# Spreading softmax gates over experts: gate folded into ScalarE's one-hot, the other one-hot built for four tokens in one VectorE compare

## The chip, the cores and the metric

The kernel is one program on one core of a Trainium2 chip. The metric is device time in microseconds (us) of one execution. TensorE (PE) does the products, VectorE (DVE), ScalarE (ACT) and GpSimd (POOL) the elementwise work and the gathers, and SyncE (SP) issues most of the transfers.

## The reference, cut to what matters

The layer mixes tokens (a gated recurrence beside a convolution) and then runs a layer of 16,384 single-neuron experts. Only the second half touches the change:

```python
sc, idx = lax.top_k(s, PEER_TOPK)                 # per head two lists of 16 keys out of 128
cand = (sc[:, :, 0, :, None] + sc[:, :, 1, None, :]).reshape(T, PEER_HEADS, 256)
top_sc, pos = lax.top_k(cand, PEER_TOPK)          # 16 experts i * 128 + j per head
eidx = jnp.take_along_axis(cidx, pos, axis=-1)
gate = jax.nn.softmax(top_sc, axis=-1)
...
act = jax.nn.gelu(jnp.einsum('thkd,td->thk', u_tab[eb], hb), approximate=False)
y   = jnp.einsum('thk,thkd->td', gb * act, v_tab[eb])
```

1,024 tokens, 8 heads, 16 experts per head: 128 (expert, gate) pairs for each token. All other input shapes are 1,024 features wide.

## The kernel before

**Two ways through the experts.** The 1,024 tokens are 8 blocks of 128. Blocks 3 and 7 (`GATHERED`) fetch their experts' rows by indirect DMA. Blocks 0, 1, 2, 4 and 5 (`DENSE`) compute all experts with matrix products and multiply the result by a dense table of gates. Block 6 (`MIXED`) gathers the rows of the first table, and its gates, already multiplied by the gelu, are spread like those of the dense blocks for the second product. The dense part goes over all 128 groups of experts in two passes: tokens of blocks 0 to 2 first, then 4 to 6.

**Spreading.** `spread` turns the 128 pairs (i, j, gate) of each token of a block into a dense table `wd[.., j, i, token]`. It transposes the three lists so that the pair is on the partition and the token in the free dimension (`tr`: part 0 is i, part 1 is j, part 2 is the gate). Then, for four tokens at a time (a group; 32 groups per block), it builds two one-hot matrices [pair, 128] for each token: `oj` on ACT (line 989: the distance |iota - j|; line 992: Relu(1 - distance), once for all four tokens) and `oi` on DVE (line 990: compare iota with i, times the gate, once per token). PE multiplies them (line 982), into one PSUM bank (`gps`) for the four tokens; ACT copies the bank into `wt` (line 974), and after four groups SP sends `wt` to `wd` in DRAM (line 976). `oj` and `oi` have two buffers each, `wt` has one. The dense part reads `wd` back eight expert groups at a time (`wgrp`, line 1161).

**Order.** Spreading is work beside the main work: a generator that emits a group per step, and `tick` calls a fraction of a step between matrix products (`RATE_PICK`, `RATE_PICK_END`). Its instructions get a later priority (`LATER`), and a scheduler with its own estimate of durations then fixes the order on each engine. At run time every engine executes its list in order. Blocks 0 to 2 are spread while the second half of the tokens is in the recurrence, the convolution's output, the merge, the second norm and the query products; blocks 4, 5 and then 6 are spread during the first dense pass. The first dense pass may not read `wd` before all of blocks 0 to 2 stand in it (`side.until`).

**The dense part's own needs.** For every group of experts ACT and DVE split two weight tiles into a high and a low part (lines 301 and 302), ACT takes the gelu out of the only `ups` bank (line 1086), DVE multiplies it by the gates (line 1091), and PE runs 24 products into `ups` and 6 per token block into `y` (lines 1078 to 1080, 1108 to 1112).

Of the kernel before, what the change touches and what calls it, by code (L numbers as in the profile page):

```python
# [8 lines left out]
F32 = mybir.dt.float32  # L9
# [4 lines left out]
AF = mybir.ActivationFunctionType  # L14
OP = mybir.AluOpType
# [66 lines left out]
class Side:  # L82
    """Work emitted a few steps at a time between the steps of other work, and how urgent it is beside that."""
# [38 lines left out]
def layer_kernel(tc, a, out):  # L122
# [18 lines left out]
    def tick():  # L141
        """A step of the work beside, its vector instructions kept behind the main work of a few steps ago."""
        code = nc.cur_bb.bb.instructions
        n = len(code)
        for i in range(n - 1, seen[0] - 1, -1):
            if code[i].engine == mybir.EngineType.DVE:
                beats.append(code[i].name)
                break
        side.tick()
        if len(beats) == BEATS:  # L150
            for ins in code[n:]:
                if ins.engine == mybir.EngineType.DVE:
                    tc.add_manual_dep(ins, beats[0], mybir.DependencyInfo(
                        mybir.DependencyClass.NoSync, mybir.DependencyReason.DATA), reason="pace")
        rec.tick()
        norm.tick()
        tail.tick()
        due[0] = min(due[0] + TAP_RATE, 2.0)
        work_taps(int(due[0]))
        due[0] -= int(due[0])  # L160
        seen[0] = len(code)

    ctx = ExitStack()
    with ctx:
# [13 lines left out]
        def bank():  # L178
            """A PSUM bank for side work."""
            turn[0] += 1  # L180
            return spare[turn[0] % len(spare)].tile([P, 4, P], F32, name="gps")

# [23 lines left out]
        def rstd_of(ssq, n, scale, tag):  # L206
            """1 / sqrt(scale * ssq + EPS): a first guess from the exponent, then Newton steps."""
            m = small.tile([P, n], F32, name=tag + "m")
            nc.vector.tensor_scalar(m, ssq, -0.5 * scale, -0.5 * EPS, op0=OP.mult, op1=OP.add)
            t = small.tile([P, n], F32, name=tag + "t")  # L210
            r = small.tile([P, n], F32, name=tag + "r")
            ti, ri = t.bitcast(I32), r.bitcast(I32)
            nc.vector.tensor_single_scalar(ti, m.bitcast(I32), 1, op=OP.arith_shift_right)
            nc.vector.tensor_scalar(ri, ti, -1.0, float(0x5F3759DF - (1 << 30) - (1 << 22)), op0=OP.mult, op1=OP.add)
            for _ in range(3):
                nc.vector.tensor_mul(t, m, r)
                nc.vector.tensor_mul(t, t, r)
                nc.vector.scalar_tensor_tensor(r, t, 1.5, r, op0=OP.add, op1=OP.mult)
            return r

        # lower bounds of the forget gates
# [18 lines left out]
        def ada(js, cols=None):  # L240
            """Parts js of the conditioning: as rows in DRAM, or with features on the partitions of cols."""
# [62 lines left out]
        def transpose_split(pp, src, hi, lo, b):  # L304
            """src [tokens, features] -> token block b of hi, lo [feature, k, tokens]."""
            for k0 in range(0, KB, 4):
                ps = pp.tile([P, 4, P], F32, name="hps")
                for k in range(4):
                    nc.tensor.transpose(ps[:, k], src[:, P * (k0 + k):P * (k0 + k + 1)], ident)
                d = (slice(None), slice(k0, k0 + 4), slice(P * b, P * b + P))  # L310
                split(hi[d], lo[d], ps)
# [12 lines left out]
        class Mm:  # L324
            """Products with streamed weights, 256 columns at a time, in two halves of the contraction."""
# [38 lines left out]
            def weights(self, name, i):  # L364
                """The planned weights that come next; those after them are made ready a product later."""
                if not self.ready:
                    self.prepare()
                n, j, r = self.ready.popleft()
                assert (n, j) == (name, i)
                self.ahead = not self.ready  # L370
                return r

            def mm3(self, ps, l, r, step):
                """ps = sum over k of l(part, k)^T r(part, k) in three exact-product passes."""
                for k in range(KB):
                    nc.tensor.matmul(ps, l(0, k), r(0, k), start=k == 0, stop=False)
                    nc.tensor.matmul(ps, l(0, k), r(1, k), start=False, stop=False)
                    nc.tensor.matmul(ps, l(1, k), r(0, k), start=False, stop=k == KB - 1)
                    if k % step == step - 1:
                        tick()  # L380
                if self.ahead:
                    self.ahead = False
                    self.prepare()

            def feat(self, w, m, act):
                """Output features 128 m.. on partitions, tokens free."""
# [6 lines left out]
            def halves(self, w, act):  # L393
                """As feat for both m, the first half of the tokens first."""
# [7 lines left out]
            def tok(self, ws, bs, act):  # L402
                """Tokens of block b on partitions, 256 output features, for (w, b) of ws, bs."""
# [6 lines left out]
        def normed(M, where, raw):  # L410
            """The normalised input, features on partitions."""
# [14 lines left out]
        def modulate(raw, u, cols):  # L426
            """The modulated input in two parts."""
# [15 lines left out]
        def conv_in(M, cp, u, g):  # L443
            """The gated input of the convolution; its taps are left to be worked off later."""
# [29 lines left out]
        def conv_norm(M, cp, c):  # L474
            """Layer norm and swish of the convolution's output for a chunk, in DRAM."""
# [37 lines left out]
        def parts(where, src, c, name):  # L513
            """A chunk of src in two parts."""
# [22 lines left out]
        def merge(M, where, c, mg):  # L537
            """The gated sum of the branches for a chunk: mg, in two parts."""
# [15 lines left out]
        def out_norm(M, c, mg, u2):  # L554
            """The first residual sum of a chunk, and its norm and modulation: u2, in two parts."""
# [41 lines left out]
        def project(M, hp, g, u):  # L597
            """q, f, v and the output gate of two heads for a chunk, in turn."""
# [25 lines left out]
        def recurs(M, hp, c, u, between):  # L624
            """The recurrence for a chunk, two heads at a time; the last ones are left as work beside."""
# [12 lines left out]
        def recur(M, hp, g, c, z, scanm):  # L638
            """The recurrence of two heads over a chunk's tokens, its norm and gate."""
# [18 lines left out]
            # the diagonal of the scores, and zeros elsewhere  # L658
# [13 lines left out]
            # from each even token to the next: the same sums on all partitions  # L672
# [15 lines left out]
            # within each group of 2h tokens: from its first half to its second  # L688
# [21 lines left out]
            # q exp(b) in qk, k exp(b_last - b) in e  # L710
# [53 lines left out]
            # per-head norm, gate, back to features on partitions  # L764
# [25 lines left out]
        def topk(vals, idx, src, work):  # L790
            """The 16 largest of src's rows in order, and where they stand."""
# [6 lines left out]
        def ask(M, c, u2):  # L798
            """Query projection, key scores and the top 16 of each list, for a chunk."""
# [25 lines left out]
        def select(sp, b, sv, si):  # L825
            """The lists i, j of the block's experts i * 128 + j and their gates: [tokens, heads * 16]."""
# [31 lines left out]
            # which row and column of the candidates' triangle each place is  # L858
# [7 lines left out]
            def lookup(dst, one, x, hs):  # L866
                """sum over a of one[a] * (list x's entry a)"""
# [46 lines left out]
        def line():  # L914
            """A tile as long as a token's features."""
# [9 lines left out]
        def gather_u(b):  # L925
            """gate * gelu(u . h) with the rows of peer_u gathered for each token."""
# [17 lines left out]
        def gather_v(b):  # L944
            """The block's weighted rows of peer_v, gathered for each token."""
# [14 lines left out]
        def spread(sp, b, ij, w):  # L960
            """wd[.., j, i, token] = sum of w over the token's experts i * 128 + j."""
# [4 lines left out]
            nc.vector.tensor_copy(tr, ps[:, :3])  # L966
            yield
            hot = out_ = wt = None
            for n in range(P // 4 + 2):
# [14 lines left out]
                if n < P // 4:  # L984
                    oj = sp.tile([P, 4, P], F32, name="oj", bufs=2)
                    oi = sp.tile([P, 4, P], F32, name="oi", bufs=2)
                    for x in range(4):
                        t = 4 * n + x
                        nc.scalar.activation(oj[:, x], iota, AF.Abs, bias=tr[:, 1, t:t + 1], scale=-1.0)
                        nc.vector.tensor_scalar(oi[:, x], iota, tr[:, 0, t:t + 1], tr[:, 2, t:t + 1],  # L990
                                                op0=OP.is_equal, op1=OP.mult)
                    nc.scalar.activation(oj, oj, AF.Relu, bias=1.0, scale=-1.0)
# [7 lines left out]
        def pick(res):  # L1000
            """Side work: from the top lists of all blocks to the dense weights of their experts."""
# [19 lines left out]
        def gather():  # L1021
            """Side work: what is gathered for each token."""
# [14 lines left out]
        def dense(fc, gathers):  # L1037
            """All experts in turn for the tokens of a pass, weighted by wd: their rows of peer_v, summed in PSUM."""
# [23 lines left out]
            def tokens(p):  # L1062
                """Features of the tokens of pass p."""
# [6 lines left out]
            def dots(s):  # L1070
                """u . h of the experts i * 128 .. (on partitions)."""
# [50 lines left out]
            def close():  # L1122
                """The last steps, a block of tokens after the other, and what follows them."""
# [171 lines left out]
def prepare(i):  # L1295
    """The arrays as the kernel reads them, and constants that depend on shapes alone."""
# [47 lines left out]
```

## Time and profile before

| what | value |
|---|---|
| median of 3 runs | 3755.42 us (3749.34 to 3763.02) |
| span of the profiled execution | 3746.1 us |
| median of the runs above that span | 9.3 us |
| PE busy | 3610.6 us, 96% |
| DVE busy | 3157.9 us, 84% |
| ACT busy | 1849.1 us, 49% |
| spreading, first line 990 to last | 1169.3 to 2668.3 us |

The runs' times include what lies around the span; no separate time of the profiled execution is recorded, so its own time is taken as the span, and the step to the runs is the 9.3 us in the table. Busy times are unions: instructions of one engine overlap by about a tenth of a microsecond, so busy time over count is less than the mean duration of one. A PE that is shown busy is not at its peak rate, but it waits for nobody. The granted clock (PEclk) is given as a share of full speed: 1.00 is 2.4 GHz, and a lower mean of a window means that part of it ran at 1.2 GHz.

### The profile page before, as it was taken

To read this page: it belongs to the slowest core of one execution; us is meant where nothing else is said; L and a number is where in the kernel's file an instruction comes from. 1 tells how busy PE (TensorE), PEld (TensorE's weight loads), DVE (VectorE), ACT (ScalarE), POOL (GpSimd) and SP (SyncE) were. 2 spreads that over 40 slices of the span, in tenths; PEclk is the share of its full clock that TensorE was granted. 3 is DMA by queue.
4 is the path that set the end of the run, shared out by engine and by line. 5 is a ranking of instruction groups with operands and counts; after the bars stand their busy time and mean duration, and the time that the engine had idled before them with its cause. 6 is when DMAs were issued, how large, how long until landed. Compare 5 with 4: busy or idle time off the path is not lost. (4 is left out here: it accounts for less than half of the span.)

```text
span 3746.1 us, 57252 instructions
## 1 busy us (share of the span) xinstructions
PE 3610.6 (96%) x20610; PEld 3203.6 (86%) x20610; DVE 3157.9 (84%) x6739; ACT 1849.1 (49%) x3260; POOL 779.3 (21%) x652
## 2 busy tenths in 40 slices
PE   8999999899999999999999999999998999999997
PEld 5888888778899879988888899999987888888886
DVE  4999989967899966789898888898888888778888
ACT  4111355523467877644444566666534444444443
POOL 0000000000000100013333434343333333233332
PEclk9999999899999999999999999999999999999999
DMA  5222477468444778778788999999999999999996
GB/s 230 79 79 90 152 257 258 168 211 316 164 144 152 241 279 318 270 264 285 261 275 287 345 324 330 332 344 355 332 328 327 328 333 344 316 330 340 328 340 214
DMA packets 371405, 999.44 MB, mean 267 GB/s; under 512 B 30376, under 2 KB 142504, under 8 KB 360112
## 3 DMA queue, kind: packets, MB, share of 16 engines
q1 hardware_dynamic: 278960, 660.19, 50.5%
q0 software_dynamic: 92160, 335.59, 25.3%
q8 instruction: 162, 2.65, 0.3%
q14 instruction: 123, 1.01, 0.1%
HBM read 864.57 MB, written 131.09 MB: 266 GB/s over the span
## 5 line engine op out<-in xcount | busy, mean ns | idle before, releaser
L921 POOL DMA_INDIRECT gt<-in_peer_u_dram,ei x384 | 465.2, 1211 | 2139.1 <-ACT o L759 947.2
L1078 PE MATMUL ups<-u,uhi 128*128 128x384 f32 (+1 forms) x2048 | 637.8, 311 | 12.8 <-ACT act L1086 12.8
L1079 PE MATMUL ups<-u,uhi 128*128 128x384 f32 (+1 forms) x2048 | 636.2, 311 | 2.4 <-DMA u<-u2s 2.4
L1080 PE MATMUL ups<-u,ulo 128*128 128x384 f32 (+1 forms) x2048 | 635.9, 311 | 0.0
L1108 PE MATMUL y<-vhi,whi 128*128 128x512 f32 x1524 | 587.0, 394 | 12.0 <-ACT whi L301 8.0
L1109 PE MATMUL y<-vlo,whi 128*128 128x512 f32 x1524 | 589.9, 393 | 1.6 <-DVE vlo L302 1.5
L937 DVE SCALAR_TENSOR_TENSOR gt<-gt,ut 128x1024 f32<-128x1024 f32 x384 | 466.3, 1219 | 63.9 <-DMA gt<-in_peer_u_dram,ei 58.6
L1112 PE MATMUL y<-vhi,wlo 128*128 128x512 f32 x1524 | 465.7, 392 | 5.9 <-DVE wlo L302 5.9
L301 ACT ACTIVATE uhi<-uraw 128x512 fp32r<-128x512 f32 x512 | 309.9, 625 | 227.0 <-PE ups L1079 177.5
L921 POOL DMA_INDIRECT gt<-in_peer_v_dram,ei x256 | 313.1, 1223 | 515.5 <-DVE yg L953 459.9
L1078 PEld LDWEIGHTS ups<-u,uhi 128*128 128x128 f32 x2048 | 390.0, 190 | 25.6 <-ACT act L1086 16.1
L302 DVE TENSOR_TENSOR ulo<-uraw,uhi 128x512 fp32r<-128x512 f32 x512 | 346.0, 687 | 78.0 <-ACT uhi L301 76.1
L302 DVE TENSOR_TENSOR vlo<-vraw,vhi 128x1024 fp32r<-128x1024 f32 x256 | 312.8, 1222 | 110.8 <-ACT vhi L301 109.8
L1079 PEld LDWEIGHTS ups<-u,uhi 128*128 128x128 f32 x2048 | 390.1, 190 | 12.3 <-DMA u<-u2s 3.1
L1080 PEld LDWEIGHTS ups<-u,ulo 128*128 128x128 f32 x2048 | 389.8, 190 | 0.3
L301 ACT ACTIVATE vhi<-vraw 128x1024 fp32r<-128x1024 f32 x256 | 270.2, 1056 | 234.7 <-PE y L1112 140.7
L1108 PEld LDWEIGHTS y<-vhi,whi 128*128 128x128 f32 x1524 | 287.3, 189 | 68.6 <-ACT whi L301 11.4
L1112 PEld LDWEIGHTS y<-vhi,wlo 128*128 128x128 f32 x1524 | 284.9, 188 | 69.3 <-DVE wlo L302 11.0
L1109 PEld LDWEIGHTS y<-vlo,whi 128*128 128x128 f32 x1524 | 286.4, 189 | 55.2 <-DVE vlo L302 2.4
L953 DVE SCALAR_TENSOR_TENSOR yg<-gt,gate,yg 128x1024 f32<-128x1024 f32 x254 | 324.7, 1278 | 5.6 <-DMA gt<-in_peer_v_dram,ei 5.4
L301 ACT ACTIVATE whi<-wgrp 128x384 fp32r<-128x384 f32 x256 | 133.7, 522 | 352.4 <-DVE wgrp L1091 315.7
L469 DVE SCALAR_TENSOR_TENSOR y<-gl,convw,y 128x1024 f32<-128x1024 f32 x240 | 292.8, 1277 | 0.3
(298 smaller groups left out, 7460.9 us busy)
## 6 DMA issues: line engine op xcount, KB each, us to landing
uraw<-in_peer_uT_dram SPq DMA_DIRECT2D x256, 512.0 KB, 6.4
vraw<-in_peer_v_dram SPq DMA_DIRECT2D x256, 512.0 KB, 6.1
raw<-in_w_in_dram SPq DMA_DIRECT2D x96, 512.0 KB, 5.0
wd<-wt SPq DMA_DIRECT2D x48, 1024.0 KB, 6.7
wgrp<-wd SPq DMA_DIRECT2D x32, 1536.0 KB, 14.0
adaw<-in_ada_w_dram SPq DMA_DIRECT2D x24, 1024.0 KB, 8.1
raw<-in_wq_dram SPq DMA_DIRECT2D x32, 512.0 KB, 5.2
raw<-in_w_b_dram SPq DMA_DIRECT2D x16, 512.0 KB, 4.3
```

The source lines that it names most:

```text
L301: nc.scalar.activation(hi, src, AF.Copy)
L302: nc.vector.tensor_sub(lo, src, hi.bitcast(F32))
L469: nc.vector.scalar_tensor_tensor(ys[0], gl[:, j:j + S], convw[:, cb, j:j + 1], ys[0], op0=OP.mult, op1=OP.add)
L921: nc.gpsimd.indirect_dma_start(out=gt, out_offset=None, in_=a[table], in_offset=bass.IndirectOffsetOnAxis(ap=ei[:, j:j + 1], axis=0))
L937: nc.vector.scalar_tensor_tensor(gt, gt, 1.0, ut, op0=OP.mult, op1=OP.mult, accum_out=act[:, j:j + 1])
L953: nc.vector.scalar_tensor_tensor(y, gt, w[:, j:j + 1], y, op0=OP.mult, op1=OP.add)
L1078: nc.tensor.matmul(o, hi[:, k], u2[kh][:, 0, k, :m], start=kh + k == 0, stop=False)
L1079: nc.tensor.matmul(o, hi[:, k], u2[kh][:, 1, k, :m], start=False, stop=False)
L1080: nc.tensor.matmul(o, lo[:, k], u2[kh][:, 0, k, :m], start=False, stop=kh + k == 4)
L1108: nc.tensor.matmul(ys[x][dh], whi[:, r], vhi[:, c], start=first, stop=False)
L1109: nc.tensor.matmul(ys[x][dh], whi[:, r], vlo[:, c], start=False, stop=False)
L1112: nc.tensor.matmul(ys[x][dh], wlo[:, r], vhi[:, c], start=False, stop=last)
```

## The change

In `spread`, for the blocks outside `MIXED`, the second one-hot `oi` no longer carries the gate. It is a pure compare, built for the four tokens by one DVE instruction whose two inputs are broadcast (iota over the tokens, i over the 128 columns). The gate moves into `oj`: in place of one Relu(1 - d) over 128x512, ACT does four Relu(gate - gate * d) over 128x128, each with a bias and a scale read from a column of an SBUF tile (`tr[:, 2]` and the new tile `neg`, which one DVE instruction per block fills with the negated gates). The gates of those blocks are softmax values and thus positive, so the Relu still cuts every column but the right one. Block 6 keeps the old form, since its gates may be negative.

```diff
             nc.vector.tensor_copy(tr, ps[:, :3])
+            neg = sp.tile([P, P], F32, name="neg")
+            nc.vector.tensor_scalar(neg, tr[:, 2], -1.0, None, op0=OP.mult)
             yield
...
                     for x in range(4):
                         t = 4 * n + x
                         nc.scalar.activation(oj[:, x], iota, AF.Abs, bias=tr[:, 1, t:t + 1], scale=-1.0)
-                        nc.vector.tensor_scalar(oi[:, x], iota, tr[:, 0, t:t + 1], tr[:, 2, t:t + 1],
-                                                op0=OP.is_equal, op1=OP.mult)
-                    nc.scalar.activation(oj, oj, AF.Relu, bias=1.0, scale=-1.0)
+                    if b in MIXED:
+                        for x in range(4):
+                            t = 4 * n + x
+                            nc.vector.tensor_scalar(oi[:, x], iota, tr[:, 0, t:t + 1], tr[:, 2, t:t + 1],
+                                                    op0=OP.is_equal, op1=OP.mult)
+                        nc.scalar.activation(oj, oj, AF.Relu, bias=1.0, scale=-1.0)
+                    else:
+                        for x in range(4):
+                            t = 4 * n + x
+                            nc.scalar.activation(oj[:, x], oj[:, x], AF.Relu, bias=tr[:, 2, t:t + 1],
+                                                 scale=neg[:, t:t + 1])
+                        nc.vector.tensor_tensor(oi, iota[:, None, :].to_broadcast([P, 4, P]),
+                                                tr[:, 0, 4 * n:4 * n + 4, None].to_broadcast([P, 4, P]), op=OP.is_equal)
                     hot = oj, oi, 4 * n
```

The diff also empties comment and docstring lines, which changes nothing that runs.

## Rows read from the trace of the kernel before

**Rows 1.** The page: busy time, share of the span, instructions of each engine.

```profile
PE 3610.6 (96%) x20610; PEld 3203.6 (86%) x20610; DVE 3157.9 (84%) x6739; ACT 1849.1 (49%) x3260; POOL 779.3 (21%) x652
```

**Rows 2.** Windows, the two stretches that spread: length, busy time by engine, clock, DMA.

```profile
1169.00:1613.00 444.00, 421.49 (x2814) 385.44 (x2814) 349.80 (x1203) 341.25 (x756) 28.88 (x28) 0.97 0.72 256
2000.00:2680.00 680.00, 668.46 (x3697) 613.46 (x3696) 585.42 (x1096) 429.21 (x926) 269.96 (x213) 0.99 0.93 330
```

**Rows 3.** Waits of PE, 1160 to 2700 us: total, times, longest.

```profile
PE gps L982 <- ACT oj L992: 12.2, 7, 5.0
...
PE gps L982 <- ACT wt L974: 6.5, 2, 6.3
PE y L1112 <- DVE wlo L302: 5.9, 9, 1.2
...
PE gps L982 <- DVE oi L990: 2.1, 1, 2.1
```

**Rows 4.** Groups by line, 1169 to 1613 us: count, busy, mean ns, idle before.

```profile
L989 ACT ACTIVATE oj<-iota,tr 128x128 f32<-128x128 f32 x384 | 121.8, 392 | 8.9 <-DVE tr L966 4.7 <-PE gps L982 4.0
L992 ACT ACTIVATE oj<-oj 128x512 f32<-128x512 f32 x96 | 58.6, 624 | 0.2
L974 ACT ACTIVATE wt<-gps 128x512 f32<-128x512 f32 x96 | 55.4, 589 | 45.5 <-PE gps L982 25.6 <-DMA wd<-wt 19.9
...
L990 DVE TENSOR_SCALAR oi<-iota,tr 128x128 f32<-128x128 f32 x384 | 106.3, 345 | 33.9 <-PE gps L982 33.7
```

**Rows 5.** Groups by line and shape: ACT with and without a bias from SBUF.

```profile
L508 ACT ACTIVATE sq<-cv,vecs 128x512 f32<-128x512 f32 x16 | 11.1, 714 | 1.4 <-DVE cv L509 1.0 <-DVE cv L506 0.4
...
L491 ACT ACTIVATE sq<-cv 128x512 f32<-128x512 f32 x16 | 9.4, 621 | 3.5 <-PE hps L492 3.5
```

**Rows 6.** The same view: a DVE operation of two tensors, one input broadcast.

```profile
L694 DVE TENSOR_TENSOR e<-bc 128x512 f32<-128x512 f32 x48 | 32.9, 685 | 0.1
```

**Rows 7.** Windows of 20 us: PE, PEld, DVE, ACT, POOL busy, clock, DMA.

```profile
1220.00:1240.00 20.00, 20.00 (x173) 20.00 (x172) 17.54 (x49) 19.94 (x38) 4.54 (x4) 1.00 0.52 175
1240.00:1260.00 20.00, 12.28 (x93) 11.66 (x92) 18.37 (x45) 19.68 (x40) 3.97 (x4) 0.85 0.83 280
1260.00:1280.00 20.00, 20.00 (x124) 17.21 (x123) 19.32 (x47) 18.14 (x44) 4.39 (x4) 0.98 0.84 296
1280.00:1300.00 20.00, 19.67 (x133) 17.72 (x132) 20.00 (x44) 16.36 (x35) 2.09 (x2) 1.00 0.71 244
1300.00:1320.00 20.00, 20.00 (x143) 18.41 (x142) 17.20 (x33) 10.75 (x20) 1.69 (x1) 1.00 0.55 191
1340.00:1360.00 20.00, 12.87 (x68) 11.41 (x68) 8.23 (x29) 17.27 (x46) 0.00 (x0) 0.74 0.82 285
2060.00:2080.00 20.00, 13.68 (x61) 11.93 (x60) 10.46 (x21) 6.39 (x14) 4.41 (x5) 0.83 0.90 344
```

**Rows 8.** The same windows, ACT's line 992 alone: busy time, count (one per group).

```profile
1220.00:1240.00 20.00, 2.48 (x4) 1.00 0.52 175
1240.00:1260.00 20.00, 3.10 (x5) 0.85 0.83 280
1260.00:1280.00 20.00, 3.76 (x6) 0.98 0.84 296
1280.00:1300.00 20.00, 3.04 (x5) 1.00 0.71 244
1300.00:1320.00 20.00, 1.14 (x2) 1.00 0.55 191
```

**Rows 9.** Groups by line, 2000 to 2680 us: the distances of the later blocks.

```profile
L989 ACT ACTIVATE oj<-iota,tr 128x128 f32<-128x128 f32 x384 | 121.8, 391 | 21.7 <-PE gps L982 18.7 <-DVE tr L966 2.9
```

**Rows 10.** Waits over the whole span: around the transfer of `wt`.

```profile
ACT wt L974 <- DMA wd<-wt: 45.6, 20, 8.6
```

**Rows 11.** Timeline of SP: the first read of `wd` by the dense part.

```profile
1616.54 0.38 SPq L1161 DMA_DIRECT2D wgrp<-wd  x1
```

## The prediction

> **What bounds the kernel now.** I read the page first: PE is busy for 96% of the span, DVE for 84%, ACT for 49% [rows 1]. By these averages moving work from DVE to ACT looks like good balance, and PE decides the time. But an average over a program of many stages says little about two of them, so next I read windows over the stretches in which spreading runs: 1169 to 1613 us (blocks 0 to 2) and 2000 to 2680 us (blocks 4, 5, 6). In the first PE is busy for 421.5 of 444 us, DVE for 349.8 and ACT for 341.3, in the second PE for 668.5 of 680, DVE for 585.4 and ACT for 429.2 [rows 2]. So in the first stretch ACT isn't an idle engine at 49%: it is at 77%, about level with DVE. Windows of 20 us show more: from 1220 to 1260 us ACT is busy for 19.9 and 19.7 of 20 us, while DVE is at 17.5 and 18.4 [rows 7].
>
> Third, the waits of PE, since only what delays PE can move the end. From 1160 to 2700 us the largest wait of PE for another engine is for ACT's `oj` (12.2 us in 7 waits), then the copy to `wt`, also ACT (6.5 us). DVE's `oi` made it wait once, for 2.1 us [rows 3]. So the engine that is relieved is hardly waited for in spreading, and the engine that gets the work is.
>
> **The change, part by part.** 5 blocks of 32 groups take the new form: 160 groups, 96 in the first stretch (384 instructions of line 990 there, four per group [rows 4]) and 64 of the 96 groups in the second [rows 9].
>
> *DVE, removed and added.* Four compares per group are busy for 106.3 us over 384, 0.277 us each, 1.11 us per group [rows 4]. In their place stands one operation of two tensors over 128x512; the nearest row has one broadcast input and takes 0.685 us [rows 6]. The trace has none with both inputs broadcast; between no extra and the whole old price, I take the row. Saved per group: 1.11 - 0.685 = 0.42 us; 41 us in the first stretch, 27 in the second, 67 in all. Nothing at all would be saved at 1.11 us. `neg` adds five DVE operations over 128x128 for these blocks and one for block 6; at a compare's 0.277 us [rows 4] that is 1.7 us in all, and the saving covers it; without that cover it would be 1.7 us of DVE.
>
> *ACT, removed and added.* One Relu over 128x512 is busy for 58.6 / 96 = 0.610 us [rows 4]. The four new ones over 128x128 are like the distances of line 989, which read a bias from SBUF: 121.8 / 384 = 0.317 us each [rows 4]. But they also read their scale from SBUF, and no row has both. What one such operand costs is to be seen: the same shape takes 714 ns with a bias from SBUF and 621 without [rows 5], 0.093 us. So a new Relu costs between 0.317 (the second operand is free) and 0.410 us. I take the upper end, since the first operand's price was paid in full. Added per group: 4 x 0.410 - 0.610 = 1.03 us; at the lower end 4 x 0.317 - 0.610 = 0.66.
>
> The Trainium skill ("ScalarE: Activation LUTs", section "What ACT_TABLE_LOAD costs") says that each pointer operand of an ACTIVATE adds about 93 ns; for the second one no run here shows it, and by the page the sum would be the upper end.
>
> In all ACT gets 160 x 1.03 = 165 us more (106 at the lower end), against the 67 that DVE is spared.
>
> *Where the added work lies.* In the second stretch 64 x 1.03 = 66 us go into an ACT that is idle for 680 - 429 = 251 us [rows 2]. What hides it is PE's own pace; if ACT had no room there, it would be 66 us. PE's gelu bank is single, so a gelu that waits behind the Relus may still cost something: I put 1 us (0 to 4).
>
> In the first stretch 96 x 1.03 = 99 us meet 444 - 341.3 = 102.7 us of idle ACT [rows 2], and 45.5 us of that idle time are waits for PE and for the `wt` transfer [rows 4]. ACT would be full. At the lower end it is 63 us, and ACT is at 91%. Nor is the room where the work is. From 1220 to 1300 us ACT is idle for 0.06 + 0.32 + 1.86 + 3.64 = 5.9 us [rows 7], and 4 + 5 + 6 + 5 = 20 groups are in these windows [rows 8]. 20 x 1.03 = 20.6 us of added work leave ACT 14.7 us behind at 1300 us (20 x 0.66 = 13.2, and 7.3 behind, at the lower end). From 1300 to 1320 there are 9.25 us of idle time and 2 groups [rows 7, 8], so 7.2 us are made up, and the rest in the later windows.
>
> What queues behind the added instructions on ACT: the evictions of the recurrence's and the convolution's products and the splits of weights, for which PE waits, and the copy to `wt`, for which SP's transfer to `wd` waits and behind it, in SP's order, the loads of weights. `wt` has one buffer, and its copies already waited 45.6 us for transfers [rows 10]; each time ACT now has more to catch up on.
>
> How much of the 14.7 us reaches PE? Between nothing and all. Nothing, if the scheduler lets spreading slip behind the main work, which its later priority allows; the added work would then only have to be done before the dense part first reads `wd` at 1616 us [rows 11]. All, if PE's list keeps its products of `oj` and `oi` where they are. For a value between, the trace has a hint: from 1220 to 1260 us ACT was full and PE still waited by name for `oj` for only a part of the idle 7.7 us of 1240 to 1260 [rows 7]. So the scheduler copes in part. I take half, 7 us.
>
> *What DVE's relief gives back.* PE's waits for DVE in this whole stretch are those for `wlo` and `oi`, 5.9 + 2.1 us [rows 3]. The second goes at best, and part of the first: 0 to 5 us, and I take 1, since PE's main waits have other causes.
>
> *Removed dependences.* A product now waits for one compare of all four tokens, and for a Relu of its own token; before it was the other way round. The first product may start 0.2 us sooner after ACT's work begins, the last one 1.03 us later. That is within the 7 us.
>
> **Sum.** +7 +1 -1 = +7 us against the profiled span: 3746.1 + 7 = 3753 us. The median of the runs lies 9.3 us above that span, so the same step from it gives 3755.4 + 7 = 3762 us, 0.2% more. A measurement here can tell about 0.3% (11 us) from no change, so the forecast is "no change that can be told", leaning to slower.
>
> The Trainium skill ("ScalarE: Activation LUTs", section "Rules for kernel authors") says that Relu, products and the like belong on VectorE rather than ScalarE. By that rule the whole move is for the worse, which is the first rival; the trace bears it out in that a one-hot piece takes 0.277 us on DVE and 0.317 or more on ACT [rows 4].
>
> **Rivals.** *Slower, because ACT becomes the bound of the first stretch.* Place: 1220 to 1520 us. All 14.7 us reach PE, and an idle PE also loses clock: in 1240 to 1260 us 7.7 idle us go with a mean clock of 0.85, 0.15 x 20 = 3 us of full speed lost; in 1340 to 1360 us 7.1 with 0.74, 5.2 us [rows 7]. At 0.4 us per idle us, 14.7 becomes 20.6, plus 1 for the second stretch: 3755.4 + 22 = 3777 us. It decides from about 8 us of new idle time in PE (8 x 1.4 = 11). For it speaks that ACT's added work fills the stretch's idle time, against it that spreading may slip and that PE's named waits for `oj` were small when ACT was full.
>
> *Faster, because DVE was what held the first stretch.* DVE is at 17.5 to 20.0 of 20 us from 1220 to 1300 [rows 7], and 20 groups there free 20 x 0.42 = 8.4 us. If that lets the chains through DVE run ahead, the idle time and the clock lost in 1240 to 1260 go, 7.7 + 3 = 11 us, and a few of the 6.3 idle us at 2060 to 2080 [rows 7]: 14 us in all, 3755.4 - 14 = 3741 us. Against it: DVE's `oi` was waited for 2.1 us only [rows 3], and the stall at 1340 to 1360 came with DVE busy for 8.2 of 20 us. But any change of the instructions lets the scheduler place everything anew, and the stalls at 1340 and at 2060, worth 12 and 10 us with their lost clock, can go or others appear.
>
> *The change doesn't do what it says.* If a compare with two broadcast inputs took 1.1 us or more, DVE would gain nothing and ACT would still pay: the -1 goes, 3763 us, which isn't told from the forecast.
>
> **Chances and range.** Forecast, with the last rival: 0.44. Slower by more than 11 us: 0.36. Faster by more than 11 us: 0.20, mostly for the placing anew. The likeliest case's own range is 3748 to 3767 us (the unknown operand price and the share that reaches PE, 0 to 8 us of stall with its clock). The range to hold the time 8 times in 10 takes in both others: 3742 to 3786 us; the upper end is for the 14.7 us in full and as much again from the later waits around `wt`, 3755.4 + 1 + 2 x 14.7.
>
> **What the profile after would show.** If the prices are right: Relu of 128x128 at about 0.48 us in its mean (392 + 93 ns), 160 compares of 128x512 at about 0.69 us, DVE's busy time down by some 65 us and ACT's up by 165. If the mechanism is right: ACT at over 95% from 1169 to 1613 us, PE's waits for `oj` above the 12.2 us of before, in the first stretch, and none of note after 2100 us, where PE keeps its pace. Wrong would be: spreading that is finished at the same time with ACT well below full (the second operand is free), PE's idle time in the first stretch smaller than 444 - 421.5 = 22.5 us [rows 2], or a change of time that arises where nothing is spread.

## The result, and the profile after

| kernel | median of the runs (lowest to highest) | ratio to the kernel before, 95% interval |
|---|---|---|
| before | 3752.38 us (3745.97 to 3763.02, 4 runs) | |
| after | 3784.73 us (3782.84 to 3786.45, 4 runs) | 1.0081 [1.0063, 1.0099] |

The change costs 32 us, 0.8%. The span of the profiled execution is 3784.3 us, 38.2 us above that of before. The runs of the kernel after take 1.8 us more than their span. By that step the profiled execution of before took about 3748 us, some 4 us under its kernel's median here, so a few of the 38.2 belong to it and not to the change. The 9.3 us between its span and the median of its runs are mostly this difference between executions.

The page after, the row that answers to [rows 1]:

```profile
PE 3636.3 (96%) x20610; PEld 3224.1 (85%) x20610; DVE 3102.5 (82%) x6265; ACT 2001.2 (53%) x3738; POOL 771.7 (20%) x652
```

ACT has 152 us more and DVE 55 us less. The groups by line after, 1169 to 1650 us, which hold all 96 groups of blocks 0 to 2 as the shorter window of [rows 4] does:

```profile
L1001 ACT ACTIVATE oj<-oj,tr,neg 128x128 f32<-128x128 f32 x384 | 162.7, 488 | 1.4 <-DVE neg L968 1.4
...
L991 ACT ACTIVATE oj<-iota,tr 128x128 f32<-128x128 f32 x384 | 123.3, 395 | 13.5 <-PE gps L984 12.4 <-DVE tr L966 1.1
L1003 DVE TENSOR_TENSOR oi<-iota,tr 128x512 f32<-128x512 f32 x96 | 65.7, 686 | 54.8 <-PE gps L984 54.5 <-issue 0.2
L976 ACT ACTIVATE wt<-gps 128x512 f32<-128x512 f32 x96 | 55.6, 588 | 20.3 <-PE gps L984 16.8 <-DMA wd<-wt 3.5
```

A folded Relu is busy for 162.7 / 384 = 0.424 us, the compare for 0.684. The prices are close to the forecast ones. Note the window: before, the last of these groups ended at 1611 us, now at 1650.

The windows after. The first and third answer to [rows 2]:

```profile
1169.00:1613.00 444.00, 418.40 (x2704) 380.40 (x2703) 304.67 (x869) 402.22 (x959) 32.69 (x28) 0.95 0.70 251
1613.00:1660.00 47.00, 33.96 (x168) 29.08 (x166) 31.30 (x147) 39.17 (x96) 4.03 (x3) 0.78 0.54 195
2000.00:2680.00 680.00, 671.04 (x3695) 616.55 (x3694) 564.53 (x928) 487.69 (x1106) 252.87 (x207) 0.99 0.92 327
```

The window of the kernel before for the second of these rows:

```profile
1613.00:1660.00 47.00, 43.85 (x226) 39.76 (x225) 42.17 (x170) 20.90 (x32) 7.74 (x8) 1.00 1.01 329
```

The third row after is as good as before (671.0 busy, 668.5 before), although ACT has 58 us more in it. In the first, PE is idle for only 3 us more, but at a lower granted clock (0.95, before 0.97), and it got through 2704 matrix products where it had done 2814. Then comes a stretch with 13 idle us and a granted clock of 0.78, where the kernel before had 3 and 1.00. PE's waits after, 1160 to 1700 us (total, times, longest):

```profile
PE gps L984 <- ACT oj L1001: 15.5, 15, 4.6
PE gps L984 <- DVE oi L1003: 5.8, 2, 3.8
PE ups L1090 <- ACT act L1098: 3.6, 1, 3.6
PE acc L376 <- ACT qt L811: 3.2, 1, 3.2
PE gps L984 <- ACT wt L976: 2.6, 2, 2.3
```

Named waits for `oj` grew by 3.3 us only [rows 3]. They can't explain 32 us. What does is seen when three moments are laid beside each other: the end of the main work (the last copy of a query product, `qt`), the end of spreading for the first pass (the 96th copy to `wt`), and the start of the dense part (its first gelu, `act`). The timeline of ACT before (start, duration, what, idle time before it in brackets):

```profile
1610.92 0.60 ACT L974 ACTIVATE wt<-gps 128x512 f32<-128x512 f32 x1 [0.30 <-PE gps L982]
...
1616.40 0.60 ACT L811 ACTIVATE qt<-acc 128x512 f32<-128x512 f32 x1 [1.58 <-PE acc L378]
...
1622.35 0.49 ACT L1086 ACTIVATE act<-ups 128x384 f32<-128x384 f32 x1
```

The timeline of ACT after; its first two rows are the last copies of blocks 0 and 1:

```profile
1346.55 0.60 ACT L976 ACTIVATE wt<-gps 128x512 f32<-128x512 f32 x1 [1.68 <-PE gps L984]
...
1501.08 0.60 ACT L976 ACTIVATE wt<-gps 128x512 f32<-128x512 f32 x1
...
1625.36 0.60 ACT L811 ACTIVATE qt<-acc 128x512 f32<-128x512 f32 x1 [0.95 <-PE acc L378]
...
1649.98 0.60 ACT L976 ACTIVATE wt<-gps 128x512 f32<-128x512 f32 x1 [0.53 <-PE gps L984]
...
1659.85 0.49 ACT L1098 ACTIVATE act<-ups 128x384 f32<-128x384 f32 x1
```

Before, spreading ended 5.5 us ahead of the main work, and the dense part began 6 us behind the main work. After, the main work is 9 us later, but spreading ends 24.6 us behind it, and the dense part's first gelu comes 9.9 us behind spreading.

What held the dense part is seen at its first product on PE (`ups`). The timeline of PE before:

```profile
1616.20 0.33 PE L1078 MATMUL ups<-u,uhi 128*128 128x384 f32 x1
```

The timelines of PE and of DVE after:

```profile
1650.63 0.69 PE L1090 MATMUL ups<-u,uhi 128*128 128x384 f32 x1 [0.69 <-ACT wt L976]
...
1664.15 0.56 DVE L1103 TENSOR_TENSOR wgrp<-wgrp,act 128x384 f32<-128x384 f32 x1 [3.44 <-DMA wgrp<-wd]
```

Before, this product came right behind the main work's last ones, 4.7 us after spreading's last copy had ended (1610.92 + 0.60 us). After, PE stood idle until that copy was through (1649.98 + 0.60) and began 0.05 us behind it. So it isn't the gates in `wd` that the dense part waited for at its start: they are first used at 1664.15 us, 4.3 us after the first gelu had begun. PE's list has the dense part's first product behind spreading's last group.

The dense part starts 37.5 us later, and from there to the end of the span the two profiled executions take the same time (2123.7 us before, 2124.5 after).

### The profile page after: what moved, and what is told of

It reads as the page before. It is cut to its first block, busy times and chain, and to the rows that moved or that the text cites. A ratio compares the mean times of both kernels' runs of the same rounds, so it can differ in the third digit from the quotient of the medians.

```text
span 3784.3 us, 57277 instructions
## 1 busy us (share of the span) xinstructions
PE 3636.3 (96%) x20610; PEld 3224.1 (85%) x20610; DVE 3102.5 (82%) x6265; ACT 2001.2 (53%) x3738; POOL 771.7 (20%) x652
## 5 line engine op out<-in xcount | busy, mean ns | idle before, releaser
L937 DVE SCALAR_TENSOR_TENSOR gt<-gt,ut 128x1024 f32<-128x1024 f32 x384 | 466.5, 1220 | 68.9 <-DMA gt<-in_peer_u_dram,ei 68.2
```

The costliest lines, as they stand in the source:

```text
L937: nc.vector.scalar_tensor_tensor(gt, gt, 1.0, ut, op0=OP.mult, op1=OP.mult, accum_out=act[:, j:j + 1])
```

## The experiments

Times are medians of runs. There were three sets, each on a chip of its own with the kernel before beside it (medians of 3753.66, 3758.60 and 3755.28 us), and each ratio is taken within its set. For each the three moments were read from ACT's timeline of its profiled execution, each from the first copy of a query product on (901.3 us before, 902.4 to 908.2 in the others), so that what differs in the hundreds of microseconds ahead of spreading is left out. The table gives how much later than in the kernel before each comes; "rest" is the change of the time from the first gelu to the end of the span.

| kernel | ratio | block 0 spread | block 1 | block 2 | main work | first gelu | rest |
|---|---|---|---|---|---|---|---|
| before (us from the first copy) | | 415.5 | 553.2 | 709.6 | 715.1 | 721.1 | 2123.7 |
| after | 1.0081 | +28.7 | +45.5 | +37.9 | +7.8 | +36.3 | +0.8 |
| e2, new form in blocks 0 to 2 | 1.0115 | +26.8 | +42.7 | +35.0 | +5.1 | +33.4 | +11.4 |
| e8, in blocks 0 and 1 | 1.0111 | +28.2 | +48.0 | +38.9 | +10.3 | +37.0 | +9.3 |
| e7, in block 0 | 1.0043 | +22.6 | +15.8 | +17.9 | +2.1 | +14.9 | +14.8 |
| e1, in blocks 4 and 5 | 1.0041 | -4.0 | -5.3 | +0.3 | +3.5 | +3.4 | +2.5 |
| e4, the fold alone | 1.0110 | +26.7 | +40.8 | +37.3 | +9.5 | +35.1 | +12.6 |
| e3, the merged compare alone | 1.0033 | +9.2 | +7.9 | +9.8 | +2.5 | +6.4 | +4.7 |
| e5, Relus with one SBUF operand | 1.0034 | +12.3 | +15.2 | +7.9 | +0.6 | +3.4 | +17.0 |
| e6, `neg` alone | 1.0039 | -0.5 | +0.5 | +6.3 | +9.5 | +9.4 | +12.8 |
| n1, `neg` in late blocks alone | 0.9999 | 0.0 | +0.9 | +0.9 | +0.9 | +0.9 | +4.5 |
| i4, late blocks, one operand, no `neg` | 1.0006 | +0.5 | +0.1 | +0.4 | +0.4 | +0.4 | +1.8 |
| i1, GpSimd makes the distances | 1.0094 | +18.0 | +14.2 | +1.8 | +35.5 | +35.4 | +4.8 |
| i3, DVE makes both one-hots | 1.0068 | +3.9 | -26.1 | -58.4 | +14.5 | +12.7 | +13.0 |

Each row is one profiled execution. "Rest" scatters by some 15 us among kernels whose dense part is the same, so it isn't read further. It is not small beside the loss itself, so a row's first gelu doesn't give its ratio us by us. Over the whole table the two go together: the kernels whose first gelu is over 33 us late lose 0.8 to 1.2%, the others 0.7% at most.

### Where in the program: e2 and e1

In the kernel after, e1 keeps the old form in the early blocks, e2 in the late ones (`NB` is 4):

```diff
-                    if b in MIXED:
+                    if b in MIXED or b < NB:      # e1
+                    if b in MIXED or b >= NB:     # e2
```

> The new form for blocks 4 and 5 only; blocks 0 to 2 keep the old one. Theory (ACT is full in the first stretch, and what it can't do there is paid before the dense part can start): within 0.3% of the kernel before, 3752 us or so, since ACT has room in the second stretch; the first use of wd by the dense part at about 1631 us, as before. Rival 1 (the cost lies with every block, for instance gelus that wait behind the Relus in the dense part, or instructions placed anew): 64 of 160 groups, so about 0.4 of the 32 us, +13 us, 3765 us.

> The new form for blocks 0 to 2 only; blocks 4 and 5 keep the old one. Theory: the whole loss or nearly, +28 to +33 us (3780 to 3785 us), the first use of wd at about 1664 us instead of 1631. Rival 1: 96 of 160 groups, +19 us, 3771 us.

Measured: e1 3769.77 us, 1.0041 [1.0026, 1.0055]; e2 3795.35 us, 1.0115 [1.0097, 1.0134]. The early blocks alone cost as much as the whole change, or more; rival 1 had 3771 us for them, 24 less. e1 missed its theory: it isn't free, and its time alone is what rival 1 had for it. Its dense part starts when that of before does, within 3.4 us, but its profiled execution was its fastest, 12 us under its median, and so doesn't show the 0.4%. e6 below tells what that is.

### Which half of the edit: e3 and e4

e3 takes the fold back (old Relu over four tokens) and keeps the merged compare; it leaves the gate out and so computes another function. e4 keeps the fold and compares token by token.

```diff
-                        for x in range(4):
-                            t = 4 * n + x
-                            nc.scalar.activation(oj[:, x], oj[:, x], AF.Relu, bias=tr[:, 2, t:t + 1],
-                                                 scale=neg[:, t:t + 1])
+                        nc.scalar.activation(oj, oj, AF.Relu, bias=1.0, scale=-1.0)    # e3
...
-                        nc.vector.tensor_tensor(oi, iota[:, None, :].to_broadcast([P, 4, P]),
-                                                tr[:, 0, 4 * n:4 * n + 4, None].to_broadcast([P, 4, P]), op=OP.is_equal)
+                        for x in range(4):    # e4
+                            t = 4 * n + x
+                            nc.vector.tensor_scalar(oi[:, x], iota, tr[:, 0, t:t + 1], None, op0=OP.is_equal)
```

> Only VectorE's part, for all five blocks: one compare for four tokens, and one Relu(1 - d) over 128x512 as before. The gate is left out of wd for these blocks, so the output is that of another function; the work on every other engine is that of the kernel before. Theory (ACT's added work is the cause): not slower than before, 3742 to 3757 us. Rival 2 (one compare for four tokens makes PE's products wait for the whole group): slower by a good part of the 32 us, over 3765 us.

> Only ScalarE's part, for all five blocks: four Relus with the gate as bias and scale, and four compares per group on VectorE as before, without the product with the gate there. Theory: the whole loss, +28 to +38 us (3780 to 3790 us), the upper part if DVE's lost relief of 0.42 us per group matters. Rival 2: most of the loss is gone, under 3765 us.

Measured: e3 3764.74 us, 1.0033 [1.0021, 1.0045]; e4 3798.45 us, 1.0110 [1.0092, 1.0128]. The fold is the expensive half; e4 lies 8 us above its theory. The merged compare wins nothing alone: e3 lies between its theory and its rival. Whether the merge is worth anything beside the fold isn't shown: after has 1.0081 and e4 1.0110, the intervals touch, the two start their dense part within 1.2 us of each other, and e2, which has the merge in its early blocks, has 1.0115. The compare of e4 also shows what the merge saves. The group of e4, 1169 to 1613 us:

```profile
L1005 DVE TENSOR_SCALAR oi<-iota,tr 128x128 f32<-128x128 f32 x348 | 75.4, 281 | 45.9 <-PE gps L984 45.7
```

Without the gate a compare is busy for 75.4 / 348 = 0.217 us instead of 0.277 [rows 4]. So of the 0.42 us saved per group, 0.24 come from dropping the gate and 0.18 from the merge.

### The second operand: e5

```diff
-                                                 scale=neg[:, t:t + 1])
+                                                 scale=-1.0)
```

Relu(gate - d) is still zero off the right column, as d is 1 or more there.

> The changed kernel with a constant scale (-1) in the four Relus, the gate as their bias only: one operand from SBUF instead of two. The spread value is then Relu(gate - distance), still the gate in the right column as gates are below 1 and distances whole numbers. Theory (ACT's added time in the first stretch sets the loss): 96 x 4 x 0.093 = 36 us less ACT work there, so most of the 37 us that the dense part starts late is gone: 3757 to 3768 us, first use of wd at 1635 to 1648 us. Rival 3 (it is the number of ACT instructions and the finer waits, not their time): 3778 us or more.

Measured: 3772.54 us, 1.0034 [1.0022, 1.0046]. Its Relus by line (minimum, median, maximum in ns, first and last start):

```profile
L1001 ACT ACTIVATE oj<-oj,tr x640: 381/392/413, 1180.8 to 2485.5; 128x128 f32<-128x128 f32 x160
```

The same row of the kernel after:

```profile
L1001 ACT ACTIVATE oj<-oj,tr,neg x640: 473/484/517, 1176.8 to 2495.8; 128x128 f32<-128x128 f32 x160
```

The second operand costs 484 - 392 = 92 ns, or 35 us over the 384 early Relus. Taking it out makes spreading's end come 30 us sooner (+7.9 in place of +37.9), and the dense part starts 33 us sooner, at nearly its old place. Two thirds of the fold's ACT work is still there (0.66 us per group, 63 us in the three blocks) and costs next to nothing at the dense part's start. The timeline of ACT in e5, the three moments:

```profile
1622.21 0.60 ACT L811 ACTIVATE qt<-acc 128x512 f32<-128x512 f32 x1
...
1624.04 0.59 ACT L976 ACTIVATE wt<-gps 128x512 f32<-128x512 f32 x1
...
1630.92 0.49 ACT L1098 ACTIVATE act<-ups 128x384 f32<-128x384 f32 x1
```

The time falls by less, from 1.0081 to 1.0034, about 18 us, and stays above the theory's 3768 us: e5's "rest" is 17.0 us longer than that of before, and why isn't known.

### Does it add up by blocks: e7 and e8

```diff
-                    if b in MIXED:
+                    if b:           # e7: new form in block 0 alone
+                    if b > 1:       # e8: in blocks 0 and 1
```

> The changed kernel with the new form for block 0 only: 33 us of added ACT work, at the start of the first stretch, with two blocks to make it up. Theory (ACT's added time counts only as far as the first stretch's idle ACT time doesn't hold it): no more than what placing anew has cost (about 13 us), 3755 to 3772 us, first use of wd before 1650 us. Rival (each block that takes the new form costs a third of the 33 to 37 us, on top of what placing anew costs): 3778 us.

> The new form for blocks 0 and 1 only: 66 us of added ACT work against 103 us of idle ACT time, of which 45 are waits in spreading itself. Theory: between, first use of wd at 1640 to 1660 us, 3762 to 3782 us; the step from two blocks to three is the largest. Rival (in proportion): two thirds of the loss of blocks 0 to 2, 3780 us.

Measured: e7 3775.98 us, 1.0043 [1.0027, 1.0058]; e8 3799.41 us, 1.0111 [1.0094, 1.0127]. e7 lies between its theory and its rival. e8 is slower than both its theory and its rival had it, and my expectation that the third block would cost the most was wrong: two blocks cost as much as three. The lag arises in blocks 0 and 1 (+28.2, then +48.0) and block 2 makes up 8 to 9 us whichever form it has (e8 -9.1, after -7.6). So it isn't the sum of the added ACT time that counts: e8 adds 66 us in two blocks and starts its dense part 37 us late, e5 adds 63 us in three and starts it 3.4 us late. The timeline of ACT in e8, the same three moments:

```profile
1633.59 0.58 ACT L811 ACTIVATE qt<-acc 128x512 f32<-128x512 f32 x1
...
1656.75 0.60 ACT L976 ACTIVATE wt<-gps 128x512 f32<-128x512 f32 x1 [0.77 <-PE gps L984]
...
1666.23 0.49 ACT L1098 ACTIVATE act<-ups 128x384 f32<-128x384 f32 x1
```

Again the dense part's first gelu follows spreading, by 9.5 us, and its first product on PE starts 0.05 us behind the end of the last copy, at 1657.40 us. Why block 2, where ACT's added work is gone in e8, makes up no more of the lag is open: its last copies still wait for PE (`gps`), whose order was fixed beforehand.

### What any edit costs: e6, n1, i4

e6 is the kernel before with the six `neg` instructions, which nothing reads; n1 has them for the late blocks only; i4 has the new form in blocks 4 and 5, with e5's constant scale, and no `neg` at all.

```diff
+            neg = sp.tile([P, P], F32, name="neg")                                # e6; n1: under "if b >= NB:"
+            nc.vector.tensor_scalar(neg, tr[:, 2], -1.0, None, op0=OP.mult)
```

> The kernel before with the one DVE operation per block that negates the gates, whose result nothing reads; 6 operations of about 0.28 us. It asks what placing anew costs by itself, since blocks 4 and 5 alone and the compare alone each came out 11 to 16 us slower than before. If those are due to the scheduler's other order, this one may differ by as much as 15 us in either direction, with the loss in the first stretch, 1160 to 1640 us. If they are costs of the new instructions themselves, it is within 5 us of the kernel before, 3748 to 3758 us.

> The kernel before with the negation of the gates for blocks 4, 5 and 6 only (three DVE operations whose result nothing reads). The first stretch should be that of the kernel before; what is placed anew lies in the dense passes. If the order of the dense passes matters as much as e6's later half suggests: up to +12 us, 3750 to 3770 us, all of it after 2000 us. If not: within 5 us of before.

> The part of the change that ACT has room for, at its lowest price: blocks 4 and 5 only, Relu(gate - d) with a constant scale and no negated gates; blocks 0 to 2 and the order of the first stretch as before. VectorE is spared 27 us in the second stretch and ACT gets 42 us. Theory (PE sets the pace there, DVE's relief has nothing to give): within 0.3% of before, 3742 to 3765 us; a gain over 11 us would show that DVE did hold PE there.

Measured: e6 3772.40 us, 1.0039 [1.0024, 1.0053]; n1 3757.39 us, 0.9999 [0.9989, 1.0009]; i4 3757.59 us, 1.0006 [0.9995, 1.0017]. Three short DVE instructions in the first stretch, unread, cost 0.4%; those of the second stretch cost nothing. The timeline of ACT in e6:

```profile
1623.14 0.60 ACT L976 ACTIVATE wt<-gps 128x512 f32<-128x512 f32 x1 [0.30 <-PE gps L984]
...
1631.83 0.60 ACT L811 ACTIVATE qt<-acc 128x512 f32<-128x512 f32 x1
...
1637.71 0.49 ACT L1088 ACTIVATE act<-ups 128x384 f32<-128x384 f32 x1
```

Here spreading is in time and it is the main work that ends late (+9.5), with the first gelu 5.9 us behind it. Three instructions of 0.22 us can't take 9 us themselves. The traces show what else is new: the order. In n1 and i4, PE and ACT execute the same instructions in the same order as in the kernel before, up to 1690 us and more. In e6 PE's order differs from its 6229th product on, at 1167 us, and ACT's from 1185 us. And e1 has e6's order on both engines up to 1700 us, and e6's time (1.0041 beside 1.0039). So the 0.4% of both goes with the order that the scheduler makes when `neg` is in the early blocks. That the order is the cause is still argued, as no run holds it fixed. The pair also shows how far single profiles scatter: with one order, e1's main work is 3.5 us late and e6's 9.5, and spreading 0.3 and 6.3.

The variants of the change fall into three levels. Without `neg` in the early blocks: 1.000 (n1, i4). With it, and at most one block of the full fold: 1.0033 to 1.0043 (e1, e3, e5, e6, e7). With it and the full fold in two blocks or three: 1.0081 to 1.0115 (after, e2, e4, e8). So 0.3 to 0.4% need not come from what e1, e3, e5 or e7 compute; e6 has it for nothing.

### Less work on ACT: i1 and i3

Both start from the kernel before and alter `oj` in the early blocks. i1 lets GpSimd subtract for four tokens at once, then ACT takes Abs and Relu over 128x512; i3 makes `oj` with one DVE compare for four tokens, without ACT.

```diff
+                    if early:    # i1; the Abs per token goes, the Relu stays
+                        nc.gpsimd.tensor_tensor(oj, iota[:, None, :].to_broadcast([P, 4, P]),
+                                                tr[:, 1, 4 * n:4 * n + 4, None].to_broadcast([P, 4, P]), op=OP.subtract)
+                        nc.scalar.activation(oj, oj, AF.Abs)
...
+                    if early:    # i3; Abs and Relu go
+                        nc.vector.tensor_tensor(oj, iota[:, None, :].to_broadcast([P, 4, P]),
+                                          tr[:, 1, 4 * n:4 * n + 4, None].to_broadcast([P, 4, P]), op=OP.is_equal)
```

> The kernel before, but for blocks 0 to 2 GpSimd subtracts iota and j for four tokens in one operation, and ACT takes the absolute value and the Relu once per group over 128x512: 2 x 0.61 instead of 1.88 us, 0.66 us per group less, 63 us less ACT work in the first stretch, where GpSimd is busy for 29 of 444 us. Theory (ACT is the scarce engine of the first stretch): 3735 to 3752 us. Rival (GpSimd slows VectorE or its products come late): slower than before.

> The kernel before, but for blocks 0 to 2 the one-hot oj is built on VectorE too, by one compare for four tokens, and ACT builds none: ACT 1.88 us per group less (180 us in the first stretch), VectorE 0.69 more (66 us, which makes it 416 of 444 us busy). If only ACT's load counts: faster, 3725 to 3745 us. If any engine that is nearly full costs the same, VectorE takes ACT's place: 3752 to 3785 us.

Measured: i1 3794.09 us, 1.0094 [1.0075, 1.0112]; i3 3783.07 us, 1.0068 [1.0051, 1.0085]. In both spreading is in time (i3: 58 us early) and the main work is late, by 35.5 and 14.5 us. The window of i3's first stretch:

```profile
1169.00:1613.00 444.00, 414.83 (x2772) 378.46 (x2771) 395.70 (x1222) 188.91 (x275) 29.91 (x27) 0.97 0.72 257
```

DVE is busy for 396 of 444 us and ACT for 189. Emptying ACT doesn't help if DVE fills: PE's named waits for DVE from 1160 to 1680 us are 21.5 us in i1 and 17.1 in i3, where the kernel before has 3.1, and the main work is late. i1's theory failed, and i3 came as its second case had it. PE's order in both also differs from that of the kernel before, from 1167 us on, and what that costs by itself isn't known. No version beat the kernel before.

## Where the prediction was right, and where it was wrong

**The time.** The likeliest case, 3762 us within 3748 to 3767, did not come. The measured 3784.73 lies in the range for 8 times in 10, 1.3 us under its upper end, and that is luck: the upper end stood for a backlog of 14.7 us and as much again from waits around `wt`, and neither is what happened. The faster rival's 3741 us lay just outside the range that was said to hold it.

**Prices: right.** Forecast were about 0.48 us for a folded Relu in its mean, 0.410 busy, and about 0.69 for the compare; the rows show 0.484 to 0.488, 0.424 and 0.686. The Trainium skill ("ScalarE: Activation LUTs", section "What ACT_TABLE_LOAD costs") gives 93 ns for each pointer operand; the runs agree with it for the second one too, at 92 ns (484 against 392 in e5). ACT grew by 152 us where 165 were forecast, DVE fell by 55 where some 65 were.

**The second stretch: right.** It was to cost 1 us. From the first gelu to the end the kernel after takes 0.8 us more in its one profile. e1, which has the full form in blocks 4 and 5, measures as e6 does (1.0041 and 1.0039), which has e1's order up to there and no new form at all. i4, which adds 42 of the 66 us, measures 1.0006.

**DVE's relief: 1 us was taken, and none is seen alone.** In the first stretch PE's named waits for `oi` went from none to 5.8 us (the 2.1 us of [rows 3] lie after 2000 us), and e3 gains nothing. What the merged compare is worth beside the fold (e4 against after) is not settled.

**The backlog and what it costs: wrong, and this decides.** Two steps of it failed. First, "7.2 us are made up, and the rest in the later windows". I counted any idle ACT time as room for the backlog. Block 0, with 33 us added, is 28.7 us late at its end, and block 1 brings it to 45.5. The reading that fits, though no run tests it alone: part of ACT's idle time lies within spreading's own chain (a distance waits until PE has freed `oj`, a copy to `wt` until PE has filled `gps`), and work that is late moves that idle time along instead of filling it. Such idle time was on view: 25.6 of the 45.5 us ahead of the copies to `wt` were waits for PE [rows 4]; the rows after still show 12.4 and 16.8 us of them. ACT was at 402 of 444 us, 91% and not "over 95%", and yet late. Second, "Nothing, if the scheduler lets spreading slip behind the main work". I gave the slip a due time, 1616 us [rows 11], but not the margin against it, and I took the reading of `wd` for what falls due. What falls due is the dense part's first product on PE, which starts at the later of two moments: the main work's last products there, and the end of spreading's last copy. Before, the copy ended 4.7 us ahead of it, and this was the margin. Spreading's slip was 37.9 us, so 33.2 came through, and the first group then took 3.1 us longer to its gelu (9.2 us in place of 6.2; the clock granted was 0.50 from 1640 to 1650 us and 0.56 to 1655, and 1.00 from 1616 to 1622 before): 36.3 us. The term of 7 us, half of 14.7, should have been the lag of spreading at its end less 4.7 us, 33 us. The main work slipped by 7.8 us; that this is near the 7 is chance. The waits around `wt`, which I expected to grow with each catching up, fell: its copies waited 19.9 us for transfers before [rows 4] and 3.5 after.

**The slower rival** had the right engine and sign, but not the place: 3777 us was to come from waits of PE between 1220 and 1520. PE's named waits for `oj` in 1160 to 1700 are 15.5 us, 3.3 more than before. The loss lies from 1613 to 1660 us, when the main work has run out and PE has only spreading to do, at ACT's pace: 13 idle us where before there were 3, and a granted clock of 0.78 in place of 1.00, at most 0.22 x 47 = 10 us of full speed, as some of the low clock falls into idle time; the rest lies in what PE got through less before it (110 products).

**What stays open.** How much of the 0.8% is the new order that `neg` in the first stretch brings (e6: 0.4%) and how much is spreading's lag can't be had by subtraction, since the dense part's start is the later of two moments: lag hides a late main work. That the lag comes through is shown by PE's wait for the last copy, in the kernel after, e2, e4, e7 and e8, and by the levels of e5, e7 and e8; why it isn't made up in block 2 isn't. Open too is the "rest" of e5, e6 and e7, 13 to 17 us where n1 and i4 have under 5.

## What to carry to other kernels

Side work with a due time has a margin: read from the timeline when it ends, which instruction behind it stands in line for it and when that one could start otherwise, before calling a slip free. That instruction need not be the one that uses the result. Before counting idle time of an engine as room for more work, see whether what ends it is the work's own chain: here ACT was at 91%, and spreading was 38 us late. In a kernel whose order a scheduler fixes, run an edit that computes nothing beside the real one and compare the order of instructions in the traces: here such an edit moved the time by 0.4%, as much as four of the variants did.

## What was unexpected of the hardware

GpSimd made DVE slow in i1. The groups of DVE in i1, 1169 to 1613 us:

```profile
L992 DVE TENSOR_SCALAR oi<-iota,tr 128x128 f32<-128x128 f32 x384 | 150.2, 453 | 29.9 <-PE gps L982 29.9
...
L697 DVE TENSOR_TENSOR qk<-k,e 128x512 f32<-128x512 f32 x11 | 9.2, 834 | 0.0
...
L694 DVE TENSOR_TENSOR e<-bc 128x512 f32<-128x512 f32 x9 | 6.1, 679 | 0.0
...
L583 DVE TENSOR_TENSOR h<-acc,row 128x512 f32<-128x512 f32 x8 | 5.4, 680 | 3.8 <-PE acc L378 3.8
```

The groups of DVE before, the same window:

```profile
L697 DVE TENSOR_TENSOR qk<-k,e 128x512 f32<-128x512 f32 x11 | 7.6, 693 | 0.0
```

The 96 subtractions of GpSimd take 1.22 us each. In i1 the same compares take 453 ns in their mean in place of 345 [rows 4], and a product of two SBUF tiles (line 697) 834 in place of 693. The trace says which of them: 92 of the 384 compares lie at least partly beside a subtraction and take 822 ns in their mean, the other 292 take 337. Of the 11 products of line 697 the 4 beside one take 1078 ns, the others 694. The search for the largest values (line 792, one SBUF input) isn't slowed: 273 ns beside a subtraction, 13 times, and 277 otherwise. Lines 694 and 583 keep their time, but none of theirs lies beside a subtraction, so they tell nothing. The 106.3 us of compares became 150.2, which is more than the main work is late; that it is the whole cause isn't shown. The Trainium skill ("SBUF — State Buffer", section "SBUF: two separate sides") says that DVE and GpSimd lock a shared pair of SBUF ports against each other; the compares and products that took longer beside a subtraction agree with it.
